# Hybrid decoder step on Trainium2: five token blocks through three stages in turn, and a second feed-forward product with its operands exchanged

## The chip, the cores and the metric

The kernel runs on one core of one Trainium2 chip. Its engines work side by side, each in the order of its own queue: TensorE multiplies matrices (the profile's PE, its weight loads PEld), VectorE (DVE) and ScalarE (ACT) work elementwise and can read the product buffers, GpSimd (POOL) works elementwise on the on-chip memory, and SyncE (SP) issues most DMAs. The metric is the device time of one execution in microseconds, as a median of runs.

## The reference, cut to what matters

A group of 2048 prompt tokens and one of 64 sample tokens (8 sequences of 8) pass one decoder layer of width 1024, in single precision.

```python
h = rmsnorm(x)
z = h @ w_in                                  # 1024 -> 4352: r, k, v, three low-rank inputs, pooling input u, two gates
zs = z_rw + (z_prev - z_rw) * mu_shift        # token shift of the first 1792 columns
# recurrence per token t and head (8 heads of 64), state s of 64 x 64:
#   s = s * w_t + (s @ a_t) b_t^T + v_t k_t^T ;  y_t = s @ r_t
a_out = ((groupnorm(y) + bonus) * g) @ w_a_up          # 512 -> 1024
b_out = (pool(u) @ w_pool * pool_scale) @ w_b_up       # windowed means, 512 -> 1024
x = x + (sigmoid(gate_a) * a_out + sigmoid(gate_b) * b_out) @ w_o
h = rmsnorm(x)
x = x + square(relu(h @ w_ff1)) @ w_ff2                # 1024 -> 4096 -> 1024
y = rmsnorm(x)                                         # and the states of both groups are returned
```

## The kernel before

**Products.** Each single-precision factor is split into a high and a low part of the type fp32r, and a product is made of three: high x high, high x low, low x high. A weight unit is 128 x 1024 numbers (512 KB): `load_unit` (L113) brings it by DMA into one of two `raw` buffers, ScalarE casts it to the high part (L122), VectorE subtracts to get the low part (L123); four buffers of each part exist. A unit used for 128 output features over eight blocks of 128 inputs makes 8 x 3 products. An output of a product lies in a bank of 512 columns; the ring `mm` has three banks, `wk` and `ch` two each.

**Stage one** (L199 to L1072). Four blocks of 512 tokens, the second with the 64 sample tokens added. For a block, token rows are loaded, normed (`prep_rows`), transposed on TensorE (`put_rows`) into one stage buffer and split (`split_h`). `mix` makes the columns that the recurrence and the pooling need, `gates` the two gates; the order of these parts over the blocks is ORDER, "m0 m1 m2 g2 m3 g3 g0 g1", so the rows of blocks 0 and 1 are prepared a second time for their gates. Features are on the array and tokens stream, but for the values (`values`), where tokens are on the array. All results go to DRAM (`zd`, `vd`, `gd`, `pd`). The recurrence runs beside it in sub-blocks of 128 tokens (`wkv_sub`, 16, and one for the sample tokens): loads, decays, small products, a triangular solve with a round trip through DRAM, and a chain over two chunks of 64. `run_streams` puts everything in one order for TensorE: the main stream yields after each product, and a step of a sub-block is issued when an estimated clock `T.now` has passed the last step's latency, from the list LAT. Up to three sub-blocks are alive.

**Stage two** (L1074 to L1296). Three blocks of 768, 640 and 640 + 64 tokens; each width is cut in two for the products (384, 320, 352 columns). `mix_block` for all blocks: the normed recurrence and the pooling are read back, multiplied with w_a_up and w_b_up (`pab`), gated, and multiplied with w_o (`po`), there with tokens on the array and 512 features streaming, so that the sum with x is in token rows (`xr`). Rows go to DRAM as `x1d`, the transposed normed rows as `h2d`. Then `ff_block` for all blocks: in eight groups of 512 hidden features, the first product (`pf`), relu and square (L1243, L1244), the split (L1245, L1246), then the second product (`p`), again with tokens on the array and 512 features streaming, added to `acc` (L1284). Only the last block's last three token tiles (320 tokens) are made the other way round (`p_m`), added in L1263 and transposed back at the end. `out_rows` norms and stores.

The lines that set TensorE's order and the sub-blocks' times:

```python
        def issue(self, ins, cost):
            if self.on and self.prev is not None:
                tc.add_manual_dep(ins.ins, self.prev.name, ...)
            self.now += cost
...
                due = [x for i, x in enumerate(live) if x[1] <= T.now and not held(i)]
...
                        x[1] = T.now + lat
```

## Time and profile before

| | us |
|---|---|
| median of 3 runs (3282.9 to 3287.91) | 3286.28 |
| profiled execution, span from first to last instruction | 3275.8 |
| TensorE busy in that span | 3137.3 |
| VectorE busy | 1816.5 |
| ScalarE busy | 1064.9 |
| GpSimd busy | 347.6 |

The profiled execution has no time of its own beside its span. Reading: an engine's busy time is the union of its instructions. Products on TensorE are pipelined, so that a single one lasts longer than the distance to the next; their price is read from the distance. PEclk is the clock granted to TensorE, which has two levels here, 1.2 and 2.4 GHz; a mean between them is a mixture. A row's releaser, behind an arrow, is what ended the idle time before it. The DMAs moved 369.08 MB, 113 GB/s over the span.

### The profile page before, as it was taken

To read this page: it belongs to the slowest core of one execution; us is meant where nothing else is said; L and a number is where in the kernel's file an instruction comes from. 1 tells how busy PE (TensorE), PEld (TensorE's weight loads), DVE (VectorE), ACT (ScalarE), POOL (GpSimd) and SP (SyncE) were. 2 spreads that over 40 slices of the span, in tenths; PEclk is the share of its full clock that TensorE was granted. 3 is DMA by queue.
4 is the path that set the end of the run, shared out by engine and by line. 5 is a ranking of instruction groups with operands and counts; after the bars stand their busy time and mean duration, and the time that the engine had idled before them with its cause. 6 is when DMAs were issued, how large, how long until landed. Compare 5 with 4: busy or idle time off the path is not lost.

```text
span 3275.8 us, 54743 instructions
## 1 busy us (share of the span) xinstructions
PE 3137.3 (96%) x22249; PEld 2730.6 (83%) x22249; DVE 1816.5 (55%) x3514; ACT 1064.9 (33%) x1891; POOL 347.6 (11%) x510
## 2 busy tenths in 40 slices
PE   7898899999989999999999999999999999999998
PEld 6687777777667779999898888998898989999998
DVE  4687988547787864355563433434443436434434
ACT  4442433333333434323342312222232324212212
POOL 4113323202032221000000000000000000000000
PEclk9999999999989999999999999999999999999999
DMA  5443344444444545547674311222432324212212
GB/s 173 136 123 98 101 120 111 117 122 124 109 108 126 129 118 179 165 132 219 184 225 131 106 56 52 83 64 85 137 91 64 91 65 142 76 57 74 75 59 81
DMA packets 516538, 369.08 MB, mean 113 GB/s; under 512 B 141470, under 2 KB 457800, under 8 KB 516278
## 3 DMA queue, kind: packets, MB, share of 16 engines
q1 hardware_dynamic: 515150, 363.89, 38.4%
q8 instruction: 175, 2.87, 0.4%
q0 software_dynamic: 1136, 1.69, 0.2%
q14 instruction: 77, 0.63, 0.1%
HBM read 289.13 MB, written 72.09 MB: 110 GB/s over the span
## 4 chain that ended last, share of the span: by engine, by line
PE 67%; DVE 5%; DMA 3%; issue 1%; ACT 1%; SPq 1%; POOL 0%; DVEq 0%; POOLq 0%; ACTq 0%
PE pf L144 22%; PE p L144 19%; PE pi L144 7%; PE po L144 6%; PE pab L144 4%; PE p_m L144 3%; PE pv L144 1%; DMA gt<-gd 1%; PE gT L144 0%; DMA wab_3r<-in_w_b_up 0%; DMA x<-in_x_prompt 0%; DMA h2in<-h2d 0%; PE yT L147 0%; DMA wi_17r<-in_w_in 0%; DMA k9vq<-vd 0%
## 5 line engine op out<-in xcount | busy, mean ns | idle before, releaser
L1284 DVE TENSOR_TENSOR acc<-p,acc 128x512 f32<-128x512 f32 x224 | 151.7, 689 | 337.9 <-PE p L144 336.9
L122 ACT CAST w_0h<-w_0r 128x1024 fp32r<-128x1024 f32 x48 | 50.5, 1051 | 591.3 <-PE p L144 541.2
L1245 ACT CAST gh<-rl 128x384 fp32r<-128x384 f32 (+2 forms) x192 | 93.1, 486 | 162.5 <-DVE rl L1244 162.4
L1246 DVE TENSOR_TENSOR gl<-rl,gh 128x384 fp32r<-128x384 f32 (+2 forms) x192 | 100.3, 524 | 79.8 <-ACT gh L1245 79.2
L123 DVE TENSOR_TENSOR w_2l<-w_2r,w_2h 128x1024 fp32r<-128x1024 f32 x48 | 58.8, 1225 | 140.7 <-ACT w_2h L122 140.7
L144 PE MATMUL pf<-nh,w_0h 128*128 128x384 f32 (+2 forms) x384 | 123.7, 322 | 1.6 <-ACT rl L1243 1.6
L144 PE MATMUL pf<-nh,w_1h 128*128 128x384 f32 (+2 forms) x384 | 123.8, 322 | 1.4 <-ACT rl L1243 1.4
L144 PE MATMUL pf<-nl,w_3h 128*128 128x384 f32 (+2 forms) x384 | 123.7, 322 | 0.0
L144 PE MATMUL pf<-nl,w_0h 128*128 128x384 f32 (+2 forms) x384 | 123.6, 322 | 0.0
L144 PE MATMUL pf<-nl,w_2h 128*128 128x384 f32 (+2 forms) x384 | 123.6, 322 | 0.0
L144 PE MATMUL pf<-nl,w_1h 128*128 128x384 f32 (+2 forms) x384 | 123.5, 322 | 0.0
L144 PE MATMUL pf<-nh,w_2h 128*128 128x384 f32 (+2 forms) x384 | 123.5, 322 | 0.0
L144 PE MATMUL pf<-nh,w_2l 128*128 128x384 f32 (+2 forms) x384 | 123.5, 322 | 0.0
L144 PE MATMUL pf<-nh,w_3h 128*128 128x384 f32 (+2 forms) x384 | 123.5, 322 | 0.0
L144 PE MATMUL pf<-nh,w_3l 128*128 128x384 f32 (+2 forms) x384 | 123.5, 322 | 0.0
L144 PE MATMUL pf<-nh,w_1l 128*128 128x384 f32 (+2 forms) x384 | 123.5, 322 | 0.0
L144 PE MATMUL pf<-nh,w_0l 128*128 128x384 f32 (+2 forms) x384 | 120.2, 323 | 0.0
L1244 DVE TENSOR_TENSOR rl<-rl 128x384 f32<-128x384 f32 (+2 forms) x192 | 99.4, 520 | 30.9 <-ACT rl L1243 30.7
L123 DVE TENSOR_TENSOR w_3l<-w_3r,w_3h 128x1024 fp32r<-128x1024 f32 x48 | 58.8, 1225 | 76.5 <-ACT w_3h L122 76.4
L1243 ACT ACTIVATE rl<-pf 128x384 f32<-128x384 f32 (+2 forms) x192 | 87.9, 460 | 40.0 <-PE pf L144 39.9
L122 ACT CAST w_2h<-w_2r 128x1024 fp32r<-128x1024 f32 x48 | 50.4, 1049 | 153.0 <-DMA w_2r<-in_w_ff 96.7
L159 POOL TENSOR_TENSOR nf_0rs<-nf_0rs,mhalf 128x1 f32<-128x1 f32 x3 | 1.6, 550 | 862.4 <-DVE nf_0rs L158 860.1
(2478 smaller groups left out, 9910.5 us busy)
## 6 DMA issues: line engine op xcount, KB each, us to landing
w_0r<-in_w_ff SPq DMA_DIRECT2D x48, 512.0 KB
w_1r<-in_w_ff SPq DMA_DIRECT2D x48, 512.0 KB
w_2r<-in_w_ff SPq DMA_DIRECT2D x48, 512.0 KB
w_3r<-in_w_ff SPq DMA_DIRECT2D x48, 512.0 KB
x<-in_x_prompt SPq DMA_DIRECT2D x24, 512.0 KB
gd<-gt SPq DMA_DIRECT2D x48, 256.0 KB
xr<-in_x_prompt SPq DMA_DIRECT2D x16, 512.0 KB
x1d<-xr SPq DMA_DIRECT2D x16, 512.0 KB
```

What stands on the lines that cost most here:

```text
L122: S.copy(hi[:, :used], raw[:, :used])
L123: V.tensor_tensor(lo[:, :used], raw[:, :used], hi[:, :used], op=ALU.subtract)
L144: self.issue(nc.tensor.matmul(out, lhsT, rhs, start=start, stop=stop), max(passes * n / 2400.0, 0.05))
L159: T.scaled = G.tensor_tensor(rs[:sz], rs[:sz], mhalf[:sz], op=ALU.pow)
L1243: S.activation(rl[:, :sz], ps[:, :sz], AF.Relu)
L1244: V.tensor_tensor(rl[:, :sz], rl[:, :sz], rl[:, :sz], op=ALU.mult)
L1245: S.copy(gh[f][:, o:o + sz], rl[:, :sz])
L1246: V.tensor_tensor(gl[f][:, o:o + sz], rl[:, :sz], gh[f][:, o:o + sz], op=ALU.subtract)
L1284: V.tensor_tensor(acc[t][:sz, h * 512:(h + 1) * 512], ps[:sz, :], acc[t][:sz, h * 512:(h + 1) * 512], op=ALU.add)
```

## The change

The two stages become fifteen, over five blocks of 384, 448, 448, 384 + 64 and 384 tokens. A is the projection of a block, M its mixer, F its feed-forward, in the order of the new ORDER. There is one block size for all of them, and every bank holds a whole block. The recurrence keeps its arithmetic; one sub-block of 128 tokens is alive at a time, each latency but the solve's is multiplied by 1.35 (STRETCH), and it runs beside whatever stage is on. What belongs to other blocks (norming and transposing rows, adding residuals, output rows) is cut into jobs that `tick` issues between units; `flush` issues the rest, and a mixer's inputs wait for `wkv_done`. w_o and the second feed-forward product now have the features on the array and tokens streaming, and add to `acc`, which stays on chip; `add_rows` transposes it back to token rows. Where F follows M of the same block (blocks 2, 3, 4), w_o is made in two column pieces (256 and the rest, the weights loaded for each), and so are the first three units of the feed-forward. The weights are loaded for every block. Three buffers of each split part are left, and constants of the recurrence (w_decay2, w_a2, w_g2, w_pool) are loaded where they are used. `x1d` and `h2d` are gone. The diff, cut to its core:

```diff
-MPRIO = 3000
-NPRIO = 600
+NB = 448
+STRETCH = 1.35
-ORDER = "m0 m1 m2 g2 m3 g3 g0 g1"
+ORDER = "A0 A1 A2 M0 A3 F0 M1 A4 F1 M2 F2 M3 F3 M4 F4"
+HALF = 256
...
-    blocks = _blocks(TP, TS, 512, 1)
-    mblocks = _blocks(TP, TS, 768, -1)
+    blocks = _blocks(TP, TS, NB, -2)
...
-    wp = ctx.enter_context(tc.tile_pool(name="wp", bufs=4))
+    wp = ctx.enter_context(tc.tile_pool(name="wp", bufs=3))
...
-            passes = 4 if rhs.dtype == F32 else 1
-            self.issue(nc.tensor.matmul(out, lhsT, rhs, start=start, stop=stop), max(passes * n / 2400.0, 0.05))
+            cost = max(4 * n / 2400.0, 0.03) if rhs.dtype == F32 else n / 2400.0 + 0.0135
+            self.issue(nc.tensor.matmul(out, lhsT, rhs, start=start, stop=stop), cost)
...
+    def put_half(xt, o, sz, gc, hl, q, name, ring=mm_ps):
+        pv = ring(f"{name}tp{q}").rearrange("p (k t) -> p k t", k=4)
+        for j in range(4):
+            kc = 4 * q + j
+            T.transpose(pv[:, j, :sz], xt[:sz, kc * P:(kc + 1) * P], ident[:sz, :sz])
+        hh, ll = hl[0][q], hl[1][q]
+        for j in range(4):
+            g = gc[:, 4 * q + j:4 * q + j + 1]
+            S.activation(hh[:, j, o:o + sz], pv[:, j, :sz], AF.Copy, scale=g)
+            V.scalar_tensor_tensor(ll[:, j, o:o + sz], pv[:, j, :sz], g, hh[:, j, o:o + sz], op0=ALU.mult, op1=ALU.subtract)
...
+    def stage_A(b):
+        hs = hs_of.pop(b)
+        for i, m in enumerate((12, 13, 0, 1, 2, 3, 4, 5, 6, 7)):
+            if i > 2:
+                tick()
+            yield from lerp_tile(b, hs, m)
+        yield from values(b, hs)
+        ready.add(b)
+        for i, m in enumerate(range(18, 34)):
+            tick()
+            if i % 2 == 0 and i < 8:
+                pt = yield from pool_tile(b, hs, i // 2)
+                tick()
+            yield from gate_tile(b, hs, m)
+            if i % 2 and i < 8:
+                pool_mix(b, i // 2, *pt)
+        yield from flush()
...
+    def stage_M(b, after, halved):
...
+        for m in range(8):
+            tick(2)
+            wu = load_unit([w_a[:, :, m * P:(m + 1) * P], w_b[:, :, m * P:(m + 1) * P]], (8, P), f"wab{b}_{m}")
...
+        yield from flush()
+        after()
+        acc = acc_of[b] = op_.tile([P, 8, NB], F32, tag="acc", name=f"acc{b}", bufs=1)
+        cuts = [(0, HALF), (HALF, nt - HALF)] if halved else [(0, nt)]
+        parts = back_jobs(b, True) if halved else None
+        for i, (o, sz) in enumerate(cuts):
+            for m in range(8):
+                if not i or m:
+                    tick(1 if halved else 2)
+                wu = load_unit([w_o[:, :, m * P:(m + 1) * P]], (8, P), f"wo{b}_{m}_{o}")
+                ps = mm_ps(f"po{b}_{m}_{o}")
+                yield from gemm(ps[:, :sz], products(wu, ms, range(8), sz, o))
+                S.copy(acc[:, m, o:o + sz], ps[:, :sz])
+            yield from flush()
+            if halved:
+                add_jobs(parts[i])
...
+    def add_rows(xt, b, o, sz, name, ring=mm_ps):
+        acc = acc_of[b]
+        for h in range(2):
+            ps = ring(f"{name}r{h}")
+            for j in range(4):
+                T.transpose(ps[:sz, j * P:(j + 1) * P], acc[:, 4 * h + j, o:o + sz], ident)
+            V.tensor_tensor(xt[:sz, h * 512:(h + 1) * 512], ps[:sz, :], xt[:sz, h * 512:(h + 1) * 512], op=ALU.add)
...
+            if halved and g == 0:
+                held = []
+                for f in range(3):
+                    held.append(w1(f))
+                    yield from ff1(f, *held[f], 0, HALF)
+                    tick(2)
+                yield from flush()
+                for f in range(3):
+                    yield from ff1(f, *held[f], HALF, nt - HALF)
+                    act(f, held[f][1])
...
-                            for i, (x, w) in enumerate(((gh, wh), (gh, wl), (gl, wh))):
-                                T.matmul(ps[:sz, :], x[f][:, o:o + sz], w[:, 0, h * 512:(h + 1) * 512],
-                                         start=(f == 0 and i == 0), stop=(f == 3 and i == 2))
-                        V.tensor_tensor(acc[t][:sz, h * 512:(h + 1) * 512], ps[:sz, :],
-                                        acc[t][:sz, h * 512:(h + 1) * 512], op=ALU.add)
+                        for i, (w, x) in enumerate(trip(wu, j, f)):
+                            T.matmul(pss[j][:, :nt], w, x, start=(f == 0 and i == 0), stop=(f == 3 and i == 2))
+                            yield
+                    if fs[-1] == 3:
+                        m = 2 * mp + j
+                        V.tensor_tensor(acc[:, m, :nt], pss[j][:, :nt], acc[:, m, :nt], op=ALU.add)
...
+    def out_jobs(b):
+        def load(t, held):
+            o, sz, kind, src = t
+            held.append(xrow(f"xo{b}_{o}"))
+            x_rows(held[0], t)
+            for h in range(2):
+                held.append(st(f"gf{b}_{o}_{h}"))
+                D.dma_start(out=held[-1], in_=a["final_norm_g"][h * 512:(h + 1) * 512].unsqueeze(0).to_broadcast([P, 512]))
...
-                if more and len(live) < 3 and not (alone and live) and all(x[2] > 1 for x in live):
+            if cur is None and more:
+                cur = next(subs, "end")
...
-                        x[1] = T.now + lat
+                    due = T.now + STRETCH * lat
```

## Rows read from the trace of the kernel before

**Rows 1.** The page, sections 1 and 2: busy time, granted clock in 40 slices.

```profile
PE 3137.3 (96%) x22249; PEld 2730.6 (83%) x22249; DVE 1816.5 (55%) x3514; ACT 1064.9 (33%) x1891; POOL 347.6 (11%) x510
PEclk9999999999989999999999999999999999999999
```

**Rows 2.** Windows by stage: length, engines busy (instructions), granted clock, DMA share, GB/s.

```profile
0.00:22.00 22.00, 7.38 (x32) 6.41 (x32) 9.22 (x22) 10.59 (x23) 12.07 (x32) 0.89 0.57 172
22.00:1240.00 1218.00, 1112.46 (x10827) 880.97 (x10828) 899.63 (x2109) 467.73 (x893) 304.81 (x436) 0.94 0.44 120
1240.00:1770.00 530.00, 526.40 (x3260) 481.96 (x3259) 262.03 (x426) 174.85 (x289) 16.71 (x21) 1.00 0.59 178
1770.00:3267.00 1497.00, 1491.07 (x8134) 1361.25 (x8132) 641.09 (x955) 411.01 (x686) 12.99 (x22) 1.00 0.27 82
```

**Rows 3.** Chain of waits, steady products: start, length in us, instructions.

```profile
1912.94 33.31 PE pf L144 x192
2516.32 28.11 PE p L144 x120
2544.43 28.16 PE pf L144 x192
2831.28 30.79 PE pf L144 x192
```

**Rows 4.** Timeline of TensorE near 1155 us: start, length, what [idle before, releaser].

```profile
1153.21 1.04 PE L144 MATMUL k16pnb<-k16zk,selw 128*16 128x128 f32 x8
1157.97 0.47 PE L144 MATMUL k14pe<-sve,k14bkT 128*64 128x64 f32 x2 [3.06 <-DVE sve L866]
```

**Rows 5.** Timeline of VectorE in the same stretch.

```profile
1152.70 0.68 DVE L721 TENSOR_TENSOR k16WE<-k16zr,k16Pt 64x512 f32<-64x512 f32 x1
...
1156.71 0.68 DVE L724 TENSOR_TENSOR k16BK<-k16k,k16Pi 64x512 f32<-64x512 f32 x1
...
1157.51 0.41 DVE L866 TENSOR_TENSOR sve<-k14pu,k14dv 64x256 f32<-64x256 f32 x1
```

**Rows 6.** TensorE's waits: us in total, times, longest; first and last of 29.

```profile
PE k3pe L144 <- DVE sve L866: 7.5, 2, 6.0
...
PE k2pr L144 <- DVE sve L881: 0.8, 1, 0.8
```

**Rows 7.** The page, groups of instructions: busy us, mean ns, idle before.

```profile
L1284 DVE TENSOR_TENSOR acc<-p,acc 128x512 f32<-128x512 f32 x224 | 151.7, 689 | 337.9 <-PE p L144 336.9
L122 ACT CAST w_0h<-w_0r 128x1024 fp32r<-128x1024 f32 x48 | 50.5, 1051 | 591.3 <-PE p L144 541.2
...
L123 DVE TENSOR_TENSOR w_2l<-w_2r,w_2h 128x1024 fp32r<-128x1024 f32 x48 | 58.8, 1225 | 140.7 <-ACT w_2h L122 140.7
...
L1244 DVE TENSOR_TENSOR rl<-rl 128x384 f32<-128x384 f32 (+2 forms) x192 | 99.4, 520 | 30.9 <-ACT rl L1243 30.7
```

**Rows 8.** Timeline of all engines, one weight unit's way through a raw buffer.

```profile
2600.97 0.37 SPq L120 DMA_DIRECT2D w_2r<-in_w_ff  x1
...
2604.97 1.05 ACT L122 CAST w_2h<-w_2r 128x1024 fp32r<-128x1024 f32 x1 [4.34 <-DMA w_2r<-in_w_ff]
...
2606.05 1.23 DVE L123 TENSOR_TENSOR w_2l<-w_2r,w_2h 128x1024 fp32r<-128x1024 f32 x1 [3.37 <-ACT w_2h L122]
...
2607.30 0.34 SPq L120 DMA_DIRECT2D w_0r<-in_w_ff  x1
```

**Rows 9.** Windows: the stretch of the mixer stage with the most traffic.

```profile
1640.00:1690.00 50.00, 48.97 (x315) 48.60 (x314) 36.01 (x71) 21.90 (x37) 2.83 (x4) 1.00 0.84 245
```

**Rows 10.** Timeline of the end of the program.

```profile
3266.50 0.40 PE L144 MATMUL p<-w_3h,gl 128*128 128x512 f32 x1
...
3267.72 0.63 ACT L155 ACTIVATE nfj<-acc 128x512 f32<-128x512 f32 x1 [2.14 <-DVE acc L1284]
...
3270.41 0.55 POOL L159 TENSOR_TENSOR nf_256rs<-nf_256rs,mhalf 128x1 f32<-128x1 f32 x1 [3.00 <-DVE nf_256rs L158]
3271.00 1.28 DVE L1220 SCALAR_TENSOR_TENSOR acc<-acc,nf_256rs,gfb 128x1024 f32<-128x1024 f32 x1 [0.73 <-POOL nf_256rs L159]
```

More of the change, by code (lines that the diff above doesn't have):

```diff
@@ L179, in hybrid_step @@
     vsd = dr.tile([NS, LS + 1, DA], F32, name="vsd")
-    x1d = [dr.tile([n + s, DM], F32, name=f"x1d{b}") for b, (_, n, s) in enumerate(mblocks)]
-    h2d = [dr.tile([DM, n + s], F32, name=f"h2d{b}") for b, (_, n, s) in enumerate(mblocks)]
     def segs(g, n):
@@ new lines, in hybrid_step, with wkv_done, tick @@
+    G.memset(zrow[0:1, :DA], 0.0)
+    G.dma_start(out=vd[0][0:1, :], in_=zrow[0:1, :DA])
+    consts.close()
+    g2c = kp.tile([P, 8], F32, name="g2c")
+    G.dma_start(out=g2c, in_=a["norm2_g"].rearrange("(k p) -> p k", p=P))
+    consts.close()
+    ready = set()
+    done = {"p": 0, "s": False}
+    def wkv_done(b):
+        g0, n, s = blocks[b]
+        return done["p"] * P >= g0 + n and (done["s"] or not s)
+    jobs = []
+    def tick(n=1):
+        while n and jobs:
+            cond, fn = jobs[0]
+            if cond is not None and not cond():
+                return
+            jobs.pop(0)
+            fn()
+            n -= 1
@@ new lines, in col_tile, with gate_tile @@
+    def col_tile(b, hs, m, evac):
+        g0, n, s = blocks[b]
+        wu = (pre.pop(m, None) if b == 0 else None) or load_unit([w_in[:, :, m * P:(m + 1) * P]], (8, P), f"wi{b}_{m}")
+        ps = mm_ps(f"pi{b}_{m}")
+        yield from gemm(ps[:, :n + s], products(wu, hs, range(8), n + s))
+        evac(n + s, ps)
+    def gate_tile(b, hs, m):
+        g0, n, s = blocks[b]
+        gt = st(f"gt{b}_{m}")
+        yield from col_tile(b, hs, m, lambda sz, ps: S.activation(gt[:, :sz], ps[:, :sz], AF.Tanh, scale=0.5))
+        D.dma_start(out=gd[b][(m - 18) * P:(m - 17) * P, :], in_=gt[:, :n + s])
@@ new lines, in wkv_stream @@
+    def wkv_stream():
+        t0, sample = 0, False
+        while t0 < TP or not sample:
+            if not sample and SB in ready and (t0 >= blocks[SB][0] + blocks[SB][1] or t0 >= TP):
+                yield wkv_sub(None, 1, TP // P, True)
+                done["s"] = sample = True
+            elif t0 < TP and all(x[0] in ready for x in segs(t0, P)):
+                yield wkv_sub(t0, 2, t0 // P, False)
+                t0 += P
+                done["p"] += 1
+            else:
+                yield None
@@ L1046, in hybrid_step, with final_states @@
+    def final_states():
+        with tc.high_priority(offset=PRIO):
+            pt = mm_ps("pwkvT").rearrange("p (q j) -> p q j", q=4)
             for q in range(4):
```

1910 lines of the change are left out of this document (888 added, 1022 removed).

## The prediction

> **What bounds the kernel now.** I read the page first: TensorE is busy for 3137.3 us, 96% of the span [rows 1]. The span is 3275.8 us; the median of the runs, 3286.28 us, is 10.5 us longer, which is what lies around a span. I sum against the span and add 10.5. Then the windows by stage [rows 2]: before 22 us TensorE waits for the first rows; from 22 to 1240 us, where the projection and the recurrence run together, it is idle for 105.5 us of 1218 and its granted clock averages 0.94 (it falls from 2.4 to 1.2 GHz in places); from 1240 us on it is idle for 9.5 us in 2027 and the clock is 1.00. So the loss sits in the first stage: 105.5 us of idle time, and up to 0.06 x 1218 = 73 us of clock, partly the same microseconds. The rest is the number of products times their price.
>
> That price comes from the chain of waits, which merges steady stretches [rows 3]: 33.31 us for 192 products of 384 columns is 173.5 ns each; 352 columns cost 160.4, 320 cost 146.6, and 512 cost 28.11/120 = 234.2 ns. Less columns/2.4 ns, 320 to 384 carry a constant 13.5 ns, 512 carries 20.9. Counts come from the code: a unit of 8 x 3 products on 128 output features. Before: 6072 products of 512 columns (projection 2160, values 408, w_o 816, second feed-forward product 2688), 1920 of 384, 1920 of 352, 2688 of 320, 1440 of 288 (at 133.5): 1422 + 333 + 308 + 394 + 192 = 2649 us.
>
> **The change part by part.**
> *Products.* The blocks become 384, 448, 448, 384+64, 384 columns, and all but the values have the features on the array and tokens streaming. No product of 448 columns was traced. Its neighbours at equal distance give 186.7 + 13.5 = 200.2 ns (from 384) or 207.6 (from 512); I take 200.2, since three widths agree on 13.5. Each full block has 720 + 192 + 768 + 768 products (projection, branch outputs, two feed-forward products), w_o 192 more. Cut blocks (2, 3, 4) run w_o and the first three feed-forward units in pieces of 256 and 192 or 128 columns. 256 costs 120.2. For the small pieces the eight 128-column passes in 1.04 us [rows 4], 0.11 each, are the nearest floor (53 + 13.5 = 67 the other end, 22 us in all less). Sum: values 432 x 234.2 = 101; 7392 x 200.2 = 1480; 5016 x 173.5 = 870; 792 x 120.2 = 95; 792 x 0.11 = 87: 2633 us, 16 less than before. So the turned product gains little: what it saves on the 512 surcharge and on the half-empty sample tile, the cuts of w_o take back.
>
> The Trainium skill has a rule against that price: "TensorE: Matmul & The Clock Gate", section "Back-to-back issue gap", gives columns/2.4 plus 2.5 ns. By it 448 would take 189.2 and 384 162.5 ns, and the sum would be some 136 us shorter, 3119 us. The rows at 384 show 173.5 and disagree with it by 11 ns, so the rows decide; I give it under 1 in 100, inside the fast rival.
>
> *Transposes.* Both w_o and the second feed-forward product now leave features on partitions. Adding the residual needs 8 transposes per token tile, twice, in 18 tiles: 288. The tail of the old kernel had 24; the first norm was computed twice for blocks 0 and 1 (its stage buffer is single), 64 more; other tiles add 12. Net 212 x 0.11 = +23 us on TensorE [rows 4]. The memory round trips of x1d and h2d go: 34 MB that nothing waited for, worth nothing.
>
> *Recurrence.* Its arithmetic is unchanged. One sub-block is in flight instead of three, its latencies are stretched by 1.35, and it runs beside every stage. By the LAT list one takes about 107 us plus its own products, say 120, so 17 take some 2100 us, and block b's mixer, asked for at about 550, 1080, 1630, 2040, 2430 us, finds tokens ready (3, 7, 10, 13, 16 sub-blocks: 435 to 2000 us): no stage blocks on it. Of the waits, 29 rows for the recurrence sum to 71 us [rows 6]. A typical one is shown: TensorE idle 3.06 us for two 0.42 us operations [rows 4], because VectorE first does sub-block 16's work for 4 us [rows 5]. With one sub-block alive that queue is gone, but weight splits and evacuations remain: I take 71 to 24, and the other 34 us of idle time to 24. The clock: the same small products spread over nearly twice the time; of 73 us some 60 are not idle time already counted, and I take 24 to stay. Gain 47 + 10 + 36 = 93 us; bounds 30 (waits return wherever the recurrence runs) and 125.
>
> *Weights.* Five passes instead of four (projection) and three (rest): 594 units of 512 KB instead of 376, each a load on SP's queue, a cast of 1.05 us on ScalarE and a subtraction of 1.23 us on VectorE [rows 7]: +229 and +268 us. VectorE rises from 55% to some 64% of the span [rows 1]; nothing waits for an average. The loop of one raw buffer is 6.33 us from issue to next issue [rows 8]; two buffers give a unit every 3.2 us, TensorE wants one every 24 x 0.2 = 4.8 or 4.2 us. Cover: 1 to 1.6 us a unit. In the cut w_o it wants one every 2.6 to 2.9 us for 16 units; buffered units cover most: 2 us each time, 6 in all. SP waits in order for a raw buffer, so the recurrence's loads queue behind it, as before, within the 48 us set aside.
>
> *New seams.* (a) Mixer followed at once by the same block's feed-forward (three times): last w_o evacuation to the first product on the second columns is transposes, two 0.69 additions, squares at 0.63, a power at 0.55, a scale like the 1.28 of the last rows, transposes and 8 splits, 11 us for a tile and about 16 for two [rows 7, 10]; 8.6 us of cut products and 3.5 of transposes cover it. 4 left, 6 with queues: 18 us. (b) Mixer stages take the previous block's output rows in: a unit costs VectorE a split of 1.23 and four operations of about 0.6 (0.52 at 352 columns), a tile's output 2.9, the recurrence up to 2.4 ((900 - 136 x 1.23)/17 = 43 us a sub-block, a third of its 120 us), 8.9 in all against 6.7 of TensorE, for four units [rows 2, 7]; and about 13 MB in 46 us, 285 GB/s, where a stretch at 245 GB/s used 0.84 of the DMA engines [rows 9]. 4 us in each of four stages: 16. (c) The end: 8.9 us from the last product now, the last tile's addition, norm and store [rows 10]. Then three whole tiles in two row buffers: about 22. +13. (d) Splits and evacuations in the feed-forward beside the recurrence: +8, bounds 0 and 40. Sum +55; bounds 20 and 110.
>
> Total: products -16, transposes +23, recurrence -93, weights +6, seams +55: -25, span 3251, time **3261 us**.
>
> **The rivals.**
> *A, slower: 448 columns are priced like 512.* 7392 x 7.4 ns = 55 us: 3316. It decides from a surcharge of 16.9 ns, where the 25 us are gone. For: 448 is as near to 512 as to 384; against: 13.5 is constant over three widths.
> *B, slower: the weight stream becomes the bound.* It decides when the loop of 6.33 us reaches 8.3 us, two units of a 384 block. At 9.0 us, with 2.7 us of queues on ScalarE and VectorE, 228 units lose 0.34 us each: 78 us, 3339. For: VectorE at 74% in the first stage [rows 2] and one set of split buffers fewer (3 for 4); against: 6.33 measured.
> *C, slower: the waits move along with the recurrence.* Only the lower bound of 30 is gained: 3324. For: the weight splits that stand in VectorE's queue come faster; against: the wait shown was another sub-block's doing.
> *D, faster: the spreading does all it can.* Gain 125, seams 20, no stall on weights: 32 + 35 + 6 = 73 less, 3188.
> That the change doesn't do what it says would need the mixers to block on the recurrence, the last at about 2000 of its 2430 us; not likely enough for a place of its own.
>
> **How the numbers follow.** Forecast (3225 to 3285) 0.45; A 0.17; B 0.10; C 0.13; D 0.15. This kernel can be told from no change at about 0.2%, 6.6 us, 3279.7 to 3292.8. Faster: 0.38 of the forecast's and D's 0.15, 0.53; same: the forecast's upper edge and the lower ones of A and C, 0.10; slower 0.37. The range leaves out most of B and the end of D: 3180 to 3350; the forecast's own is 3225 to 3285.
>
> **What would show it.** In the profile after: steady stretches of 448 columns at 200 ns (207 is A); TensorE's waits for the recurrence's tiles summing to 20 to 30 us and the mean clock from 0.976 to about 0.99 (unchanged is C); no waits of products on split weights outside the cut stretches (else B); three idle gaps of some 6 us at feed-forward starts, and some 20 us between last product and end. The prediction is wrong if the products' steady sum isn't near 2633 us, or if the seams exceed 110 us.

## The result and the profile after

The changed kernel takes **3394.46 us** (median; 3386.16 to 3400.14) against 3284.59 us (3277.97 to 3287.91) of the kernel before on the same chip: a ratio of **1.033**, 95% interval 1.031 to 1.035. The forecast was 3261, the range ended at 3350. The span of the profiled execution grew from 3275.8 to 3389.6 us, by 114. The runs below were made on several chips, each with the kernel before beside it on the same chip (medians of 3285 to 3292 us there); the microseconds given are differences of medians, and by the ratios to the kernel before they come out up to 6 us otherwise.

The page after, sections 1 and 2 (it answers [rows 1]), with the line on the DMAs and the first line of section 4, the chain by engine:

```profile
PE 3193.5 (94%) x22853; PEld 2915.3 (86%) x22853; DVE 2083.6 (61%) x3864; ACT 1326.0 (39%) x2330; POOL 357.5 (11%) x496
PEclk9999999999999999999999999899999999998999
DMA packets 743073, 471.83 MB, mean 139 GB/s; under 512 B 140753, under 2 KB 715643, under 8 KB 742796
...
PE 45%; DVE 7%; DMA 5%; ACT 2%; issue 2%; SPq 0%; POOL 0%; DVEq 0%; POOLq 0%; ACTq 0%
```

VectorE's share rose from 55 to 61%, close to the forecast of 64. The granted clock averages 0.973 where before had 0.976. Windows by stage after, as in [rows 2] (length, engines busy with instructions, clock, DMA share, GB/s): the five mixers, and behind the last two of them the feed-forwards beside no recurrence.

```profile
644.00:747.00 103.00, 86.41 (x498) 82.15 (x497) 74.64 (x154) 42.56 (x87) 16.26 (x14) 0.92 0.53 144
...
1301.00:1416.00 115.00, 105.94 (x735) 92.13 (x734) 87.99 (x179) 50.79 (x104) 21.24 (x22) 0.96 0.58 164
...
1990.00:2147.00 157.00, 142.34 (x1205) 124.68 (x1203) 107.26 (x291) 60.70 (x121) 22.62 (x28) 0.95 0.57 159
...
2548.00:2653.00 105.00, 93.49 (x634) 88.56 (x633) 64.98 (x103) 48.16 (x88) 4.08 (x6) 0.97 0.69 206
2653.00:2978.00 325.00, 323.66 (x1681) 299.68 (x1681) 169.36 (x230) 112.26 (x169) 1.09 (x2) 1.00 0.40 119
2978.00:3086.00 108.00, 96.28 (x639) 93.99 (x638) 64.30 (x105) 48.48 (x90) 3.82 (x6) 0.89 0.67 201
3086.00:3370.00 284.00, 279.47 (x1648) 277.67 (x1647) 149.27 (x208) 98.42 (x147) 0.68 (x2) 0.99 0.38 114
```

In the kernel before the mixers and the feed-forward were the tight part: 9.5 us of idle time in 2027 [rows 2]. Now each mixer loses 9 to 17 us of idle time, and the clock falls there; block 3's feed-forward, with no recurrence beside it, is as tight as before (1.3 of 325 us). Of the 196 us of idle time (139 before) the five mixers hold 64, the first 28 and the last 20 us of the program 42; nearly all of the rest, some 85, lies in the projections and feed-forwards beside the recurrence.

Steady products, from the chain of waits, against [rows 3] (start, length, products): 206.7 and 202.7 ns for 448 columns, 174.3 for 384.

```profile
1696.70 19.84 PE p L141 x96
...
2958.30 19.46 PE p L141 x96
...
3349.77 16.73 PE p L141 x96
```

The longest of TensorE's waits after (us in total, times, longest), as in [rows 6]:

```profile
PE pab L141 <- DVE gm L657: 14.6, 8, 5.1
PE p L141 <- DVE gl L738: 13.4, 8, 4.9
PE pi L141 <- ACT zs L431: 9.4, 4, 5.8
PE n_0tp L144 <- ACT x L176: 9.4, 1, 9.4
PE n_0tp L144 <- ACT xb L176: 9.2, 3, 7.1
```

No tile of the recurrence leads the list any more. In their place stand plain products (`pab`, `p`, `pi`) and the transposes of normed rows (`n_0tp`); the single wait of 9.4 us among these is the start of the program, 8.7 before. The end, as in [rows 10]: the last instruction of TensorE, a transpose, ends at 3369.6, and the last of the three tiles still has to fetch its row of x, because its row buffer came free late (20.0 us from that transpose to the end).

```profile
3376.26 0.33 SPq L217 DMA_DIRECT2D xo<-in_x_prompt  x1
3380.91 1.29 DVE L691 TENSOR_TENSOR xo<-xo_256r,xo 128x512 f32<-128x512 f32 x2 [6.56 <-DMA xo<-in_x_prompt]
...
3385.66 0.34 SPq L794 DMA_DIRECT2D out<-xo  x1
```

To see where the 114 us went I took every distance from the start of one TensorE instruction to the start of the next, and sorted it by what the two are. A product's steady price is columns/2.4 ns plus 13.4 (17.0 at 448 columns; at 512, 20.8 before and 14.5 after; at least 110 ns); what goes over it is listed by its reason. The last three columns are experiments, described below.

| us on TensorE | before | after | before, no recurrence | after, no recurrence | after, no recurrence, no seams |
|---|---|---|---|---|---|
| up to the first instruction | 9 | 9 | 4 | 10 | 10 |
| products at their steady price | 2648 | 2656 | 2648 | 2656 | 2627 |
| products over it, clock at 1.2 GHz | 34 | 64 | 11 | 47 | 11 |
| products over it, before another product | 52 | 103 | 30 | 43 | 31 |
| products over it, before a transpose | 2 | 26 | 3 | 22 | 8 |
| transposes (how many) | 61 (469) | 131 (681) | 58 (469) | 123 (681) | 82 (393) |
| the recurrence's own | 348 | 307 | | | |
| products over it, before the recurrence's | 72 | 39 | | | |
| other | 39 | 34 | 44 | 30 | 29 |
| after the last | 9 | 20 | 9 | 16 | 13 |
| span | 3275.8 | 3389.6 | 2806.9 | 2946.2 | 2810.5 |

### The profile page after: what moved, and what is told of

Its sections match the earlier page's. It is cut to its first block, busy times and chain, and to the rows that moved or that the text cites. A ratio compares the mean times of both kernels' runs of the same rounds, so it can differ in the third digit from the quotient of the medians.

```text
span 3389.6 us, 57495 instructions
## 1 busy us (share of the span) xinstructions
PE 3193.5 (94%) x22853; PEld 2915.3 (86%) x22853; DVE 2083.6 (61%) x3864; ACT 1326.0 (39%) x2330; POOL 357.5 (11%) x496
## 4 chain that ended last, share of the span: by engine, by line
PE 45%; DVE 7%; DMA 5%; ACT 2%; issue 2%; SPq 0%; POOL 0%; DVEq 0%; POOLq 0%; ACTq 0%
PE p L141 17%; PE pf L141 16%; PE pi L141 3%; PE po L141 2%; PE pab L141 2%; DMA wo_256r<-in_w_o 1%; DMA gm<-gd 1%; DMA wo_0r<-in_w_o 1%; DVE wo_0l L158 0%; DMA out<-xo 0%; PE pv L141 0%; DVE wo_256l L158 0%; ACT wo_256h L157 0%; PE k16py L141 0%; PE gT L141 0%
## 5 line engine op out<-in xcount | busy, mean ns | idle before, releaser
L774 DVE TENSOR_TENSOR acc<-p,acc 128x448 f32<-128x448 f32 (+1 forms) x320 | 189.2, 595 | 186.2 <-PE p L141 181.9
L141 PE MATMUL p<-gl,w_0h 128*128 128x448 f32 (+1 forms) x320 | 115.4, 361 | 13.5 <-DVE gl L738 13.4
L141 PE MATMUL p<-gh,w_0h 128*128 128x448 f32 (+1 forms) x320 | 114.3, 357 | 6.8 <-ACT gh L737 6.8
L141 PE MATMUL p<-gh,w_3h 128*128 128x448 f32 (+1 forms) x320 | 113.8, 356 | 4.9 <-DVE acc L774 4.7
L141 PE MATMUL p<-gh,w_2h 128*128 128x448 f32 (+1 forms) x320 | 113.8, 355 | 4.0 <-DVE acc L774 2.4
L141 PE MATMUL p<-gh,w_1h 128*128 128x448 f32 (+1 forms) x320 | 114.4, 358 | 0.0
L141 PE MATMUL p<-gh,w_0l 128*128 128x448 f32 (+1 forms) x320 | 114.1, 357 | 0.0
L141 PE MATMUL p<-gl,w_3h 128*128 128x448 f32 (+1 forms) x320 | 113.9, 356 | 0.0
L141 PE MATMUL p<-gl,w_1h 128*128 128x448 f32 (+1 forms) x320 | 113.8, 356 | 0.0
L141 PE MATMUL p<-gh,w_1l 128*128 128x448 f32 (+1 forms) x320 | 113.7, 355 | 0.0
```

The lines of the kernel that those rows point to most:

```text
L141: self.issue(nc.tensor.matmul(out, lhsT, rhs, start=start, stop=stop), cost)
L774: V.tensor_tensor(acc[:, m, :nt], pss[j][:, :nt], acc[:, m, :nt], op=ALU.add)
```

## The experiments

**First, the two halves apart.** The recurrence left out of both kernels, `wkv_stream` issuing nothing:

```diff
     def wkv_stream():
+        return
         t0, sample = 0, False
...
-                            in_=yd[b][o:o + sz, e * 256:(e + 1) * 256]...
+                            in_=xin[:, e * 256:(e + 1) * 256]...
```

> The changed kernel with the recurrence left out (no sub-block is issued; the mixers read rows of x in place of its result, and the sample state is copied through). Without any stall the rest would take 9 (start) + 20 (end) + 2656 (products at their steady price) + 75 (681 transposes at 0.11) + 33 (other small products) = 2793 us of span, some 2803. Theory S, the stretches at the mixers and cuts lose time by themselves (weight loop, traffic, transposes in the product stream): the 346 us of recurrence on TensorE and a third of the clock loss go, the idle time of products and transposes (139 us) stays: about 3000, 190 above the same kernel before without its recurrence. Rival R, these stretches lose time because the recurrence's work now stands in their engine queues: the idle time goes with it, 2830 to 2880.

> The kernel before with the recurrence left out in the same way. From its trace: 3276 of span less 348 us of the recurrence's products and 72 us that TensorE waited for them, and most of the 34 us of products in the slow clock: 2820 to 2850. Both theories expect this; it is the yardstick for the changed kernel without recurrence. Theory S expects the difference of the two to be larger than the 109 us between the full kernels (about 150 to 190), since the recurrence's own gain of 75 us no longer covers the seams; rival R expects it to be 0 to 60.

Measured: 2935.01 and 2805.39 us (0.893, 0.890 to 0.896, and 0.852, 0.850 to 0.855, of the full kernel before). The pages, section 1, after and then before, both without recurrence:

```profile
PE 2840.9 (96%) x15293; PEld 2659.6 (90%) x15293; DVE 1474.3 (50%) x2314; ACT 1144.0 (39%) x1877; POOL 62.4 (2%) x215
```

```profile
PE 2750.5 (98%) x14689; PEld 2441.3 (87%) x14689; DVE 1200.5 (43%) x1932; ACT 897.3 (32%) x1470; POOL 71.2 (3%) x229
```

The 2935 lies between theory S (3000) and rival R (2830 to 2880), the 2805 just under what both had. The difference without recurrence is 130 us, more than the 110 of the full kernels, and less than theory S had it (150 to 190): so, by the ratios to the kernel before, the recurrence costs 461 us in the changed kernel and 485 before (443.4 and 468.9 in spans). The spreading saved some 25 us, give or take 13 by the intervals of the ratios, not 93. What else the change does, seams above all, costs some 130 by itself (139 in spans; the profiled execution without recurrence was the longest of its four, at a mean clock of 0.980 where the others had 0.983, so that by estimate some 9 us of its slow clock are its own). Both halves of the prediction were wrong, by some 70 us each.

**All seams taken away**, recurrence still out: no rows added, normed or transposed between mixer and feed-forward, nothing cut, the last gain loaded once a block.

```diff
-        ms = pair_of(f"m{b}")
+        ms = ns_of[b] = pair_of(f"m{b}")
...
-                if before[0] == "M":
-                    add_jobs(back_jobs(before[1]))
...
+        halved = False
```

> The changed kernel without the recurrence, as in the first run (2935 us), and also without its seams: nothing is added, normed or transposed between mixer and feed-forward (the feed-forward takes the mixer's gated product, so the result is another one), w_o and the first feed-forward units are uncut, and the last gain is loaded once for a block. All weights are still loaded for each of the five blocks, and all products of 448 columns stay. Floor of the first run without a stall 2803, less 32 (288 transposes) and 29 (cut products): 2742; with the stalls that the kernel before shows without its recurrence (30 + 11 + 14 us): some 2800. Theory S, the seams are all of the 130 us that separate the two kernels without the recurrence: 2770 to 2815, level with 2805. Rival W, something that all stages share (five passes over the weights, VectorE's load) takes part of it: over 2840.

Measured: 2812.24 us (2808.74 to 2815.35), level with the 2805.39 of the kernel before without recurrence. Five passes over the weights are still in it, and the waits between products and the slow clock are those of the kernel before (31 for 30 and 11 for 11 us), so the passes cost nothing where nothing else gets into their way; rival W is out. The level itself is a sum: the steady products are 21 us less than in the kernel before (2627 for 2648), and the transposes, though fewer, 24 us more (82 for 58). Page, section 1:

```profile
PE 2736.2 (97%) x14213; PEld 2555.8 (91%) x14213; DVE 1374.4 (49%) x2074; ACT 1028.3 (37%) x1595; POOL 53.4 (2%) x197
```

The last column of the table says what went: 36 us of slow clock, 41 of transposes, 14 before transposes, 12 of waits between products and 29 of cut products.

**The weights by another way**: every second unit of the feed-forward not loaded.

```diff
+                if f % 2:
+                    ps = mm_ps(f"pf{b}_{g}_{f}")
+                else:
+                    wu, ps = w1(f)
...
+                if mp % 2 == 0:
                     wu = load_unit([w_2[...
```

> The changed kernel where every second unit of the feed-forward weights is not loaded and not split, and the unit before it is used again (the result is another one): 160 loads of 512 KB, 160 casts and 160 subtractions of 1.25 us fewer, the same products. Theory W, loading the weights for every block is what costs (VectorE at 61%): the product waits in the feed-forward and the clock that they cost go down by 40 to 70 us: 3325 to 3355. Rival S, the loss sits at the mixers, cuts and transposes: 3375 to 3395.

Measured: 3385.63 us (1.031, 1.029 to 1.033): 9 us for 160 units. Theory W fell here too, and with it the prediction's rival B for the feed-forward; no run took weight loads out of the projection.

**The cuts.** First uncut, then cut but with half the weight loads in the cut passes:

```diff
-    def stage_M(b, after, halved):
+    def stage_M(b, after, follow):
+        halved = False
...
+        if follow:
+            add_jobs(back_jobs(b))
+            yield from flush()
```

> The changed kernel with w_o and the first three feed-forward units of blocks 2, 3 and 4 in one piece each (weights of w_o loaded once, the rows of the block added, normed and transposed between the mixer and the feed-forward with nothing beside them). Theory S1, the cuts themselves cost (second loading of w_o at the raw buffers' 6.3 us loop, some 15 us in each of three stages, and 264 pairs of small products at 0.23 for one at 0.204, 7 us a block): 66 us less, against 3 x 20 us for the bare norm chain: 3380 to 3400, so about the same. If the cuts cost more than the chain that they hide: under 3370. If the cuts do what they should and the loss is elsewhere: 3430 to 3460.

```diff
+                if not halved or m % 2 == 0:
                     wu = load_unit([w_o[:, :, m * P:(m + 1) * P]], (8, P), f"wo{b}_{m}_{o}")
```

> The changed kernel where in the six cut passes over w_o every second unit is not loaded and the one before it used again (the result is another one): 24 loads and splits fewer, the same products. Theory L, the loop of the two raw buffers (6.3 us, 3.15 a unit against 2.6 to 2.9 of products) bounds the cut passes: of the 33, 8 and 20 us that they take over their products' time in blocks 2, 3 and 4, 30 to 45 us go: 3350 to 3365. Rival, these passes wait for the transposes and norms put into them: 3380 to 3395.

Measured: 3366.64 us (1.023, 1.021 to 1.025) uncut, 3366.02 (1.024, 1.023 to 1.026) with half the loads. So the cut costs more than the norm chain that it hides. Its price has two parts: the small products, 29 us at their steady price (2656 for 2627), and the loads of the cut passes, where halving them gives 28 us; theory L expected 30 to 45. The chain of waits in block 4's cut pass of the changed kernel (start, length, what) is the loop of the two raw buffers, as in [rows 8], with no TensorE in it:

```profile
3039.61 3.94 DMA wo_256r<-in_w_o
...
3043.63 1.06 ACT wo_256h L157
...
3044.71 1.24 DVE wo_256l L158
3045.96 3.88 DMA wo_256r<-in_w_o
```

The loop is 6.35 us, a unit every 3.2 us, for 24 products of 0.11 to 0.12 us (2.6 to 2.9 us). The windows of the cut passes of blocks 3 and 4, in the changed kernel, and below with half the loads:

```profile
2595.00:2653.00 58.00, 51.39 (x421) 50.80 (x420) 29.33 (x44) 31.09 (x57) 1.10 (x2) 0.94 0.56 158
3022.00:3086.00 64.00, 57.07 (x418) 56.19 (x417) 31.25 (x47) 31.44 (x60) 1.10 (x2) 0.85 0.55 157
```

```profile
2590.00:2640.00 50.00, 49.18 (x422) 48.74 (x421) 20.93 (x38) 23.19 (x50) 1.10 (x2) 1.00 0.38 109
3008.00:3059.00 51.00, 48.71 (x417) 47.96 (x416) 21.51 (x39) 23.18 (x51) 1.10 (x2) 1.00 0.41 120
```

8 and 13 us less, and the clock is back at 1.00: 21 of the 28 us are in these two lines. In these two passes the waits of 4.9 and 4.1 us before transposes of normed rows are gone as well, so the weights' 28 us and what the transposes cost partly count the same waits.

**The traffic of the mixers**, the gain of the last norm not loaded:

```diff
-            for h in range(2):
-                held.append(st(f"gf{b}_{o}_{h}"))
-                D.dma_start(out=held[-1], in_=a["final_norm_g"]...)
```

> The changed kernel with the gain of the last norm left out, and with it its loading for each of the 18 token tiles (512 KB each, most of them in the mixer stages, where the DMA engines are at 0.84). Theory S2, the traffic of the mixer stages bounds them: 512 KB at 260 GB/s is 2.0 us, 15 tiles give 30 us: 3365. If the traffic is not the bound there (the queue of VectorE or the weight loop is): 3385 to 3395.

Measured: 3378.19 us (1.027, 1.025 to 1.030), 16 us less, between the two. The multiplication by the gain went with the loads, which makes 36 VectorE operations 0.50 us long instead of 0.75, 9 us in all; the run doesn't tell that from the traffic. The mixers' first halves of blocks 1, 3 and 4 got 3, 5 and 5 us shorter; that of block 2, beside the recurrence, stayed at 71 us.

**The work between mixer and feed-forward** left out, everything else kept:

```diff
-        ms = pair_of(f"m{b}")
+        ms = ns_of[b] = pair_of(f"m{b}")
...
-        parts = back_jobs(b, True) if halved else None
+        parts = [[], []]
```

> The changed kernel without what stands between the mixer and the feed-forward: the rows of x are not added, normed and transposed there, and the feed-forward takes the mixer's gated product as its input (the result is another one). 288 of the 681 transposes, 18 loads of rows and their norms are gone; the order of the stages, the cut passes and all weights stay. Theory T, transposes put into TensorE's one order cost far more than their count, because what is behind them waits for a norm chain on ScalarE, VectorE and GpSimd and the clock falls after such a gap: 288 x 0.11 = 32 us, some 28 us of gaps at these tiles and some 25 us of slow clock: 3285 to 3315. Rival, their count is all they cost and the gaps are taken by the next wait (the raw buffers' loop): 3350 to 3365.

Measured: 3324.43 us (1.012, 1.010 to 1.014), 70 us less. That is twice the 32 us of the transposes' count, and short of the 80 to 110 that theory T expected: the waits between products stay (TensorE's idle time before products rises from 86 to 110 us); what took the gaps over is not shown. So what stands between mixer and feed-forward costs about twice the length of its transposes, not three times; row loads, additions and norms went with them, and the run doesn't tell these apart.

**The recurrence's side.** In the changed kernel's trace, a step of sub-block 11 in VectorE's order, in the stretch that ends in the longest wait of a feed-forward product:

```profile
1635.26 0.68 DVE L944 TENSOR_TENSOR k11WE<-k11zr,k11Pt 64x512 f32<-64x512 f32 x1
1635.42 1.67 POOL L903 TENSOR_TENSOR k11k<-k11k,k11zk 128x512 f32<-128x512 f32 x1 [1.19 <-DVE k11k L902]
1635.95 1.70 DVE L944 TENSOR_TENSOR k11WO<-k11zr,k11Pt 64x512 f32<-64x512 f32 x1
...
1637.66 1.66 DVE L943 TENSOR_TENSOR k11WE<-k11kkn,k11Pt 64x512 f32<-64x512 f32 x1
1638.74 1.71 POOL L908 TENSOR_TENSOR k11zk<-k11zr,k11k 128x512 f32<-128x512 f32 x1
1639.33 1.66 DVE L943 TENSOR_TENSOR k11WO<-k11kkn,k11Pt 64x512 f32<-64x512 f32 x1
...
1641.63 1.68 DVE L734 TENSOR_TENSOR rl<-rl 128x448 f32<-128x448 f32 x1
1643.24 2.28 DVE L158 TENSOR_TENSOR w_2l<-w_2r,w_2h 128x1024 fp32r<-128x1024 f32 x1
...
1643.97 0.74 PE L141 MATMUL p<-gh,w_0h 128*128 128x448 f32 x1 [6.82 <-ACT gh L737]
```

The first of four like operations takes 0.68 us, the next three, beside GpSimd's, 1.66 to 1.70, and the feed-forward's square (1.68 for 0.61) and the weight split (2.28 for 1.22) stand behind it; TensorE's product waits 6.82 us. Summed over all rows, VectorE's operations are 143 us longer than the tenth percentile of their form (125 in the kernel before, 13 without the recurrence). Nine of a sub-block's steps moved to VectorE, in both kernels:

```diff
-        G.tensor_tensor(k2, k2, zk, op=ALU.mult)
+        V.tensor_tensor(k2, k2, zk, op=ALU.mult)
...
-        G.tensor_tensor(c2(yc), c2(yc), qi(vt), op=ALU.add)
+        V.tensor_tensor(c2(yc), c2(yc), qi(vt), op=ALU.add)
```

> The changed kernel with nine elementwise steps of each recurrence sub-block moved from GpSimd to VectorE (the arithmetic is the same). In the trace of the changed kernel VectorE's operations sum to 143 us more than they would at their usual lengths, and the long ones (1.66 us for 0.68) lie beside a GpSimd operation for 0.74 to 1.0 of their time; without the recurrence that excess is 13 us. Theory V, products wait beside the recurrence because GpSimd lengthens VectorE's queue: the move adds some 105 us of VectorE work and takes the 130 us of excess away, and shortens the bursts; of the 60 us of product waits and 17 us of slow clock that the recurrence adds, half go: 3340 to 3365. Rival, the burst of VectorE work itself is what products wait for, whatever GpSimd does: 3385 to 3405.

> The same move in the kernel before. There the excess is 125 us, and TensorE waits 72 us for the recurrence's tiles. Theory V: a third of these waits go, 20 to 30 us: 3255 to 3270. Rival: 3280 to 3295.

Measured: 3359.08 us (1.022, 1.020 to 1.023) after, 35 less, as theory V had it; 3273.59 us (0.996, 0.995 to 0.998) before, 13 less, under its 20 to 30. The excess falls to 45 and 44 us. The same step in the changed kernel with the move:

```profile
1617.66 0.68 DVE L944 TENSOR_TENSOR k11WE<-k11zr,k11Pt 64x512 f32<-64x512 f32 x1
1618.35 0.69 DVE L944 TENSOR_TENSOR k11WO<-k11zr,k11Pt 64x512 f32<-64x512 f32 x1
1619.05 0.68 DVE L943 TENSOR_TENSOR k11WE<-k11kkn,k11Pt 64x512 f32<-64x512 f32 x1
1619.75 0.69 DVE L943 TENSOR_TENSOR k11WO<-k11kkn,k11Pt 64x512 f32<-64x512 f32 x1
```

In the kernel before the move does not lower the waits for the recurrence's own tiles (72.6 us for 72.5): its gain is in the slow clock (22 for 34 us) and in the waits between products (46 for 52).

**One burst shortened further**, eight scalings on ScalarE:

```diff
-                V.tensor_scalar(kkn[:, q], zk[:, q], nkk[:, q:q + 1], None, op0=ALU.mult)
+                S.activation(kkn[:, q], zk[:, q], AF.Copy, scale=nkk[:, q:q + 1])
```

> The kernel before with the nine steps of a sub-block on VectorE instead of GpSimd (3273.6 us, 0.4% faster than the kernel before) and eight small scalings of a sub-block on ScalarE instead of VectorE (some 2.5 us of VectorE work in one burst). Theory V, what TensorE waits for beside the recurrence is the length of VectorE's bursts: 5 to 20 us less again, 3255 to 3268. Rival, the small scalings are not in the way or ScalarE's own queue takes their place: 3270 to 3285.

Measured: 3281.4 us (0.999, 0.9975 to 1.0004), no better than the move alone. TensorE's waits before the recurrence's products did get shorter (some 55 us by the sorting of the table, 72.6 with the move alone), and other waits took their place; whether they stem from ScalarE's queue, as the rival has it, is not shown.

**The distance between the steps** in the changed kernel: 1.0 and 1.7 for 1.35.

```diff
-STRETCH = 1.35
+STRETCH = 1.0
```

> The changed kernel with the latencies of the recurrence not stretched (1.0 for 1.35); one sub-block alive as before it. A sub-block then takes some 95 us instead of 125 and the last one ends at about 1950 us instead of 2519. Theory R, it is the spreading in time that pays: steps are issued nearer to what they need, and waits for the recurrence's tiles go up: 3405 to 3430. Rival, what a sub-block costs is its own work and the bursts that it lays on VectorE, wherever it runs: 3385 to 3400.

> The changed kernel with the latencies of the recurrence multiplied by 1.7 instead of 1.35; a sub-block then takes some 155 us and the last ends at about 2750 us, before the last mixer needs it at 2978. Theory R, the distance still pays: the 39 us of waits before its tiles and part of the product waits beside it go, 15 to 40 us: 3355 to 3380. Rival, 1.35 covers the latencies and what is left comes from bursts on VectorE and from the seams: 3385 to 3400.

Measured: 3445.38 us (1.048, 1.046 to 1.051) at 1.0 and 3442.48 (1.047, 1.045 to 1.049) at 1.7: both some 50 us more. At 1.0, 1.35 and 1.7 the waits before the recurrence's products are 59, 39 and 30 us and its own time 340, 307 and 303 us: the distance does what it is for. One sub-block alive, unstretched, has 59 and 340 us where the kernel before with three has 72 and 348: most of what the change gained at the recurrence's own tiles came with the stretching. But others pay. The longest waits at 1.7:

```profile
PE p L141 <- DVE gl L738: 28.3, 9, 7.3
PE pp L141 <- issue: 21.1, 2, 11.9
PE po L141 <- DVE h4l L188: 11.8, 1, 11.8
PE pv L141 <- DVE h2l L188: 10.2, 1, 10.2
```

Feed-forward products (`p`), the pooling's (`pp`), and products behind a norm's split (`h4l`, `h2l`) wait up to 11.9 us each. Theory R and its rival both missed: the waits move to whatever the burst lands beside.

**The same in the kernel before**: at most two sub-blocks alive, and the latencies times 1.35 (without and with the nine steps moved).

```diff
-                if more and len(live) < 3 and ...
+                if more and len(live) < 2 and ...
```

> The kernel before with at most two sub-blocks of the recurrence alive instead of three; nothing else is changed. The prediction put the 71 us of waits for the recurrence down to another sub-block's work ahead in VectorE's queue. If so, a third to a half of them go: 3250 to 3270. Rival, a step waits because of its own chain, or because of whatever burst is on VectorE, and a second one alive is enough for that: 3280 to 3300. If two are too few for the recurrence to end with the first stage (17 x 125 / 2 = 1060 us from about 110 on, of 1240): over 3300.

```diff
-                        x[1] = T.now + lat
+                        x[1] = T.now + 1.35 * lat
```

> The kernel before with every latency of the recurrence but the solve's multiplied by 1.35, as the change does it, three sub-blocks alive and nothing else changed. Theory R, the part of the change that paid is the longer distance between the steps of a sub-block, not that one alone is alive and not the new stages: in the changed kernel going from 1.0 to 1.35 took 33 us off the recurrence's time on TensorE and 20 us off the waits before it; the same here gives some 50 us: 3225 to 3255. Rival, with three alive the steps of the others fill the distance, and the waits stay: 3275 to 3295.

> The kernel before with both: nine steps of a sub-block on VectorE instead of GpSimd (13 us alone) and the latencies times 1.35. If the two gains are separate: 13 us below the run with the latencies alone, 3210 to 3245. If the shorter VectorE bursts had already taken what the longer latencies wait for: the same as that run.

Measured: 3364.53 us (1.024, 1.022 to 1.026) with two alive, 3361.91 (1.023, 1.021 to 1.025) stretched, 3332.86 (1.014, 1.012 to 1.015) stretched with the steps moved. The first is the third case of its expectation, and the second is like it, so that neither is a test of the totals: the recurrence runs past its stage, and there is nothing beside it. The windows after the projection's last product, with two alive and stretched:

```profile
1357.00:1446.00 89.00, 43.99 (x786) 37.20 (x786) 34.71 (x90) 18.08 (x43) 14.26 (x16) 0.63 0.37 100
```

```profile
1378.00:1444.00 66.00, 36.78 (x533) 30.51 (x531) 20.95 (x42) 14.37 (x33) 14.28 (x16) 0.59 0.44 130
```

They do speak on the reason that the prediction gave: TensorE's waits before the recurrence's products are 71 us with two alive and 84 stretched, where three alive had 72. Fewer sub-blocks in VectorE's queue did not shorten them. The move of the nine steps gives 29 us here.

**Three repairs at once**: the nine steps on VectorE, nothing cut, the last gain loaded once a block; then the same at 1.7.

```diff
-            for h in range(2):
-                held.append(st(f"gf{b}_{o}_{h}"))
+            for h in range(2 if not gf else 0):
+                gf.append(st(f"gf{b}_{o}_{h}"))
```

> The changed kernel with three repairs at once, none of which leaves anything out: the nine steps on VectorE instead of GpSimd, w_o and the first feed-forward units uncut, and the gain of the last norm loaded once for a block instead of once for a tile. Alone they gave 35 and 28 us, and leaving the gain out altogether 16, of which 11 loads of 14 make 12. Theory S, the losses are separate stalls in separate stretches: the sum, 75 us less, 3310 to 3330. Rival, one stall hides behind another: 3335 to 3360. Either way above the kernel before, since the uncut norm chain, the transposes and the slow clock stay.

> The changed kernel with the three repairs (steps on VectorE, nothing cut, the last gain loaded once a block: 3319 us) and the latencies times 1.7. If the distance still pays beside the repairs: 3285 to 3305, level with the kernel before. If not: 3310 to 3325.

Measured: 3318.82 us (1.011, 1.008 to 1.013), 76 less than the change: the three gains are separate, as theory S had it. At 1.7 it is 3349.73 (1.019, 1.017 to 1.020), 31 more, where it was 48 without the repairs. No version of the five-block order that computes the whole layer came below the kernel before; the kernel before with the nine steps moved is the one that beats both, by 0.4% (0.2 to 0.5).

## Why the prediction was wrong, point by point

*Products, -16 forecast, +8 in the table.* The count was right; the term mis-sized is the price of 448 columns: 203.6 ns in the mean (7392 products, 25 us more), about halfway to rival A's 207.6. The three widths that agreed on 13.5 ns did not carry to a fourth. 384 columns came out as forecast (174.3 in the row above for 173.5), and so did the small pieces. Rival A as priced (+55) did not happen, but the mark from which the prediction let it decide, a surcharge of 16.9 ns, was just reached (17.0). In its sentence on the Trainium skill, 136 us less than 3261 is 3125, not 3119.

*Transposes, +23 forecast, +70 and 24 more before them.* The count was right (681 for 469). The step that failed is "212 x 0.11": in one fixed order for TensorE a transpose of a normed row stands ahead of products that don't need it, and while it waits for its norm chain they wait too. Leaving 288 of them out, with the norms and additions around them, gave 70 us, not 32.

*Recurrence, -93 forecast, some -25.* This is the larger error. The part at its own tiles came: 348 and 72 became 307 and 39, 75 us less. But the terms "other idle 34 to 24" and "clock 60 to 24" went the other way: beside the recurrence, products wait for each other 60 us more in the changed kernel (103 for 43), 22 in the kernel before, and the slow clock that it adds is 17 and 23 us. The reason given, one sub-block's work queued behind another's, is not borne out by the run with two alive, nor by the unstretched one with a single one alive (59 us of waits, where 24 were forecast). What the runs show instead: a sub-block's burst on VectorE, made longer by GpSimd beside it, delays whoever is next, as the feed-forward's square in the rows above; moving the steps off GpSimd gave 35 us. That is rival C's mechanism (the waits move along) at about its price (30 us gained); it had a chance of 0.13, too little. How much of each wait is VectorE's queue and how much the order of TensorE stays open: every change of the latencies re-laid the whole order, and made the kernel that it was tried on slower, by 31 to 76 us.

*Weights, +6 forecast, 28 for half of the loads.* The prediction had the numbers (a unit every 3.2 us against 2.6 to 2.9) and let buffered units cover them. They don't: the loop itself is on the chain of waits there, with the norm's work on the same ScalarE and VectorE, and the clock falls on top. In the feed-forward the weight stream is covered as forecast, and rival B did not happen there.

*Seams, +55 forecast.* (c), the end, was right: 20.0 us, 11 more. (b), the mixers' first halves, right in kind (16 forecast; 16 went with the gain's loads, a part of that traffic, and the 9 us of VectorE work that went with them). (a) came at other places: the feed-forwards start with hardly a gap, but the transposes for them stop the second cut pass for 7.1, 4.9 and 4.1 us. What the sum left out is the slow clock of the seams: 36 us more without the recurrence (47 for 11, of which some 9 belong to that one execution), all of it gone when the seams are.

Together, in spans without recurrence: forecast -16 + 23 + 6 + 55 = 68 us, measured 139 (130 by medians); with it, -93 against -25.5. The tests named at the end of the prediction did their work: the steady sum came out 23 us above 2633, the mean clock did not rise, and what is left of the 139 us after products (8) and the transposes' count (23) is 108 us, where seams and weights were put at 61 and 110 was named as the limit.

## What to carry to other kernels

Work that is spread from a loose stage over tight ones is worth only what its waits there cost less: price the neighbour that stands behind each of its bursts, not the waits that it leaves. A transpose, a norm or a second pass over weights put into an in-order product stream should be priced as the longest chain that its inputs may still be in, with the clock that falls after the gap, and not as its own length. And to find which half of a large change is wrong, take the same part out of both kernels and compare the rests.

## What the runs showed of the hardware

**VectorE beside GpSimd.** A two-input VectorE operation on 64 x 512 took 0.68 us, and 1.04 to 1.78 us, 1.63 on the mean, in 54 of 272 cases, which overlap a GpSimd operation for 0.84 of their time on the mean. All 54 have both inputs in on-chip memory and began while a GpSimd operation with rows of 512 was running; 18 others of that kind were running first when GpSimd's began, and kept their 0.68 us, as the first row of the step above did. In the kernel before, 43 operations of this size with one input in a product bank lay beside such a GpSimd operation for over half of their time, and none took over 0.70 us. With the nine steps moved off GpSimd the excess of all VectorE rows falls from 143 to 45 us, and without the recurrence to 13. The Trainium skill, "GPSIMD Engine Reference", section "1. Specifications", says that GpSimd's way to the on-chip memory is shared with VectorE and that VectorE operations with two operands there contend with it; the trace agrees, and the factor here is 2.4.

**The clock in a cut pass.** In the second cut pass of block 4, without the recurrence, TensorE was busy for 29.92 of 33 us at the lower of its two levels, 1.2 GHz (windows, the granted clock third from the end; the stretch ahead of it ran at 2.4):

```profile
2596.00:2608.00 12.00, 11.72 (x105) 11.58 (x104) 7.10 (x11) 6.75 (x12) 0.55 (x1) 1.00 0.54 161
2609.00:2642.00 33.00, 29.92 (x143) 29.73 (x142) 11.67 (x24) 14.13 (x32) 0.55 (x1) 0.50 0.44 128
```

Ahead of the fall TensorE had run products of 128 columns at 110 to 120 ns and transposes between them, and then waited 0.77 us for a norm's scaling on ScalarE. The chain of waits there (start, length, what):

```profile
2607.29 1.15 ACT xb L176
2608.49 0.96 PE n_0tp L144 x4
2609.45 5.01 PE po L141 x24
```

That is 209 ns for a product that takes 110 to 120 at the upper level, so TensorE looks busy because it is slow. The pass lost the clock for 33 us at once; in the changed kernel half the weight loads kept it at 1.00 in block 4's cut passes (the windows above).

**Columns.** The steady price of 448 columns steps between runs of products (202.7 ns and 206.7 ns in the rows above), where 384 columns took 174.3 ns, and 173.5 in [rows 3]. No run tells what sets the step.
